# Layer 1 of a two-layer backbone block: the low parts of the way-out weights on one engine, and the first FFN way-out weights loaded into another tile

## The chip, the cores and the metric

The kernel runs on one core of a Trainium2 chip. The metric is the device time of one execution in microseconds (us). Below, TensorE is PE in the profile, with its weight loads as PEld; VectorE is DVE, ScalarE is ACT, GpSimd is POOL, and SyncE, whose queue issues nearly all the transfers, is SP.

## The reference

The block has two layers. Each is a mixer followed by a SwiGLU feed-forward net (FFN), and each of the two starts with an RMS norm whose scale and shift, like the gate on its output, come from a conditioning vector. 512 latent tokens and 256 context tokens pass through layer 0; layer 1 returns the latent tokens only. The model width is 1024, the FFN's hidden width 2816. The change lies in layer 1, from the mixer's output projection (the way out) to the beginning of the FFN:

```python
def finish(o):                                   # o: differential attention, 8 heads of 128
    o = _rms(o, subln_w) * (1.0 - lam_init)
    return o.reshape(o.shape[0], o.shape[1], -1) @ w_out
...
x = x + gx1 * ax                                 # ax = finish(o)
x = x + gx2 * _swiglu(_rms(x, norm_ffn_w[l]) * (1.0 + scx2) + shx2, ffn_w_in[l], ffn_w_out[l])

def _swiglu(h, w_in, w_out):
    gate, up = jnp.split(h @ w_in, 2, axis=-1)
    return (jax.nn.silu(gate) * up) @ w_out
```

## The kernel before

All products are made in three passes of reduced precision. Both operands are split into a high part (a cast) and a low part (the value minus the high part), and TensorE adds high by high, high by low and low by high. So each weight tile of 128x1024 takes three steps, all in `unit` (lines 302 to 311): SyncE loads it into a raw tile (line 305), ScalarE casts it to the high part (line 309), and another engine subtracts to get the low part (line 310). The raw tiles come from a ring of two (`raw_tile`, tag `raw`), so each load waits until the raw tile two loads earlier has been subtracted. High and low parts go into rings of eight (`whi`, `wlo`).

The code is not executed in its written order. A scheduler sets the order of the instructions on each engine and of the loads on SyncE's queue, when the program is built. Within an engine the order is then fixed: an instruction that waits holds up all behind it.

**End of layer 1's mixer.** The last head (h == 7) runs over four tiles of 128 tokens. `attend1` makes the scores `sc`, their maximum (line 643, DVE), the exponentials `e` (line 645, ACT), mixes two of them (lines 651 and 652, DVE), transposes the result (`ppt`, PE), and multiplies by the values (`av`). The head's output `o` is normed: sum of squares (line 672, ACT), a factor `rs_o` in two GpSimd steps (lines 148 and 149, in `rsqrt`), and the multiplication (line 674, DVE). While this head runs, the eight way-out weight tiles are made by `out_units`: raw tiles `wor`, parts `woh` and `wol`. Before the change their subtractions go to GpSimd and VectorE in turn, and every third raw tile has a room of its own (`opa`). `OutProj.operand` transposes `o` (`opt`, line 707), casts it into `hT` (line 708) and subtracts (line 709). `OutProj.sums` runs 24 matmuls for each half of a token tile (`ops`, lines 717 to 719). The four tiles' sums, the gated residual (lines 412 and 413) and the norms of the FFN (`norm_steps`) follow.

**The norms.** For each tile, `norm_steps` writes x times its norm factor into `nroom0` (line 278), transposes it on TensorE (`npt`, line 283, eight 128x128 blocks), applies scale and shift into `nroom1` (line 291 on DVE for the first four blocks, line 289 on ACT for the other four), and splits that into `hT` (cast at line 293; subtraction at line 294, on DVE and on GpSimd). `nroom0` and `nroom1` hold two token tiles each; they are tiles with the tags `hTc0` and `hTc1`, the place of the context's operand, which layer 1's FFN does not need.

**Start of layer 1's FFN.** The hidden columns go in 11 pairs of 128 columns. A pair p loads six weight tiles in this order: two of the gate (`wgr`), two of the up part (`wur`), two of the way out (`wdr`), all through the ring of two raw tiles before the change. For p == 0 the matmuls into `pg` and `pu` (line 750) go in two halves of 256 tokens, so that the first half can start before the norms of the last two tiles are done. Then ScalarE makes `sg` (silu, line 775), DVE multiplies (`pu`, line 777), and the product is split into `hdh` (ACT, line 418) and `hdl` (DVE, line 419) for the way-out matmuls `dps` (lines 799 to 801). Beside that, the gate row of the FFN is made once: a transpose on TensorE (`gps`, line 237), a copy on DVE (`grow`, line 239), a store to DRAM (`gmem`, line 242) and a load back as a 128x1024 tile (`g0`, line 244).

Of the kernel before, what the change touches and what calls it, by code (L numbers as in the profile page):

```python
# [10 lines left out]
F32 = mybir.dt.float32  # L11
# [7 lines left out]
P = 128  # L19
D = 1024  # L20
# [44 lines left out]
def backbone(es: ExitStack, tc: tile.TileContext, x, c, ctx, c_ctx, mod_w, mod_b, norm_mix_w, norm_ffn_w,  # L65
# [3 lines left out]
    nc = tc.nc  # L69
# [3 lines left out]
    keep = es.enter_context(tc.tile_pool(name="keep", bufs=1))  # L73
# [20 lines left out]
    def acc_tile(name, n=512, one=None):  # L94

        if one is None:
            one = turn["acc"] = 1 - turn["acc"]
        return p_1.tile([P, 512], F32, name=name, tag=f"acc{one}")[:, :n]
# [6 lines left out]
    def f32(ap):  # L105
        return ap.bitcast(F32)
# [143 lines left out]
    def ctx_room(shape, dtype, name):  # L250

        return [keep.tile(shape, dtype, name=f"{name}{j}", tag=f"hTc{j}") for j in range(2)]
# [7 lines left out]
    def cols_T(j, s0, s1):  # L260

        return hT[j][0][:, :, s0:s1] if s1 <= SEQ else hT[j][1][:, :, s0 - SEQ:s1 - SEQ]
# [38 lines left out]
    def unit(pool, views, shape, bufs, name, sub=None, new_tile=raw_tile):  # L301

        raw = new_tile(shape, name + "r")
        for dst, src in views(raw):
            nc.sync.dma_start(dst, src)
        p_hi, p_lo = pool if isinstance(pool, tuple) else (pool, pool)
        hi = p_hi.tile(shape, F32R, name=name + "h", tag="whi", bufs=bufs)
        lo = p_lo.tile(shape, F32R, name=name + "l", tag="wlo", bufs=bufs)
        nc.scalar.copy(hi, raw)  # L309
        (sub or nc.vector).tensor_sub(lo, raw, f32(hi))  # L310
        return hi, lo
# [103 lines left out]
    def split(pool, src, shape, tag, bufs):  # L415
        hi = pool.tile(shape, F32R, name=tag + "h", tag=tag + "h", bufs=bufs)
        lo = pool.tile(shape, F32R, name=tag + "l", tag=tag + "l", bufs=bufs)
        nc.scalar.copy(hi, src)
        nc.vector.tensor_sub(lo, src, f32(hi))
        return hi, lo  # L420
# [256 lines left out]
    def out_units(wp, w_out, subs=(nc.gpsimd,), rooms=(raw_tile,)):  # L677
        ws = []
        for k in range(KT):
            def views(raw, k=k):  # L680
                yield raw, w_out[0, k * P:(k + 1) * P, :]
            ws.append(unit(wp, views, [P, D], 8, "wo", subs[k % len(subs)], rooms[k % len(rooms)]))
        return ws
# [38 lines left out]
    def ffn(l, xs, ntok, wp, fp, done, mods=()):  # L722
# [5 lines left out]
        wo, hid = [], []  # L728
        for p in range(NF // 2):
            def w_in(c0, name):  # L730
                res = []
                for u in range(2):
                    def views(raw, u=u):
                        yield raw, ffn_w_in[l, u * 512:(u + 1) * 512, c0:c0 + 256].rearrange(
                            "(j p) n -> p j n", p=P)
                    res.append(unit(wp, views, [P, 4, 256], 8, name))
                return res
            wg, wu = w_in(p * 256, "wg"), w_in(FFN + p * 256, "wu")
            for j in range(2):
                def views(raw, j=j):  # L740
                    yield raw, ffn_w_out[l, (2 * p + j) * P:(2 * p + j + 1) * P, :]
                wo.append(unit(wp, views, [P, D], 8, "wd"))
            for j in range(2):
                def half(w, ps, sgs):
                    for sg in sgs:
                        for k in range(KT):
                            whi, wlo = (z[:, k % 4, j * P:(j + 1) * P] for z in w[k // 4])
                            for a, b, q in ((whi, 0, 0), (whi, 1, 1), (wlo, 0, 2)):
                                for s0, s1 in sg:
                                    nc.tensor.matmul(ps[:, s0:s1], a, cols_T(b, s0, s1)[:, k, :],  # L750
                                                     start=k == 0 and q == 0, stop=k == KT - 1 and q == 2)

                if p == 0 and ntok == NTX:

                    if j == 0:
                        both = [p_sc.tile([P, 2, 512], F32, name=name, tag="sc") for name in ("pg", "pu")]
                        for s in first_segs:
                            for j in range(2):
                                for w, ps in zip((wg, wu), both):
                                    half(w, ps[:, j], [[s]])  # L760
                        j = 0
                    pg, pu = (z[:, j] for z in both)
                elif p == 0 and j == 0:
                    pg, pu = (p_sc.tile([P, 1024], F32, name=name, tag="sc") for name in ("pg", "pu"))

                    for s in first_segs:
                        half(wg, pg, [[s]])
                        half(wu, pu, [[s]])
                else:
                    pg, pu = (p_sc.tile([P, 1024], F32, name=name, tag="sc") for name in ("pg", "pu"))  # L770
                    half(wg, pg, [segs])
                    half(wu, pu, [segs])
                pg, pu = pg[:, :n_tok], pu[:, :n_tok]
                sg = fp.tile([P, n_tok], F32, name="sg", tag="sg", bufs=1)
                nc.scalar.activation(sg, pg, AF.Silu)

                nc.vector.tensor_mul(pu, sg, pu)  # L777
                hid.append(split(fp, pu, [P, n_tok], "hd", 4))
            for i, mod in enumerate(mods[0] if p == 0 and mods else ()):
                mod_chunk(*mod, lambda shape, name: fp.tile(shape, F32, name=name, tag="mw", bufs=2), fp, f"tr{i % 2}", room=("ma", 4))  # L780
            if p and mods and mods[p]:
                mod_chunks_by_pool(mods[p], fp)
            if g is None:
                g = [gate_row(l, 5, i, fp) for i in range(2 if ntok > NTX else 1)]
            if p == NF // 2 - 2:

                continue
            nj = len(hid)
            for t in CTX_FIRST[:ntok] if ntok > NTX else range(ntok):
                for n in range(2):  # L790
                    if nj > 2:
                        ps = acc_tile("dps")
                    else:
                        turn["sum"] = (turn["sum"] + 1) % 4
                        ps = p_1.tile([P, 512], F32, name="dps", tag=("acc0", "tr0", "acc1", "tr1")[turn["sum"]])
                    for j in range(nj):
                        hh, hl = (z[:, t * P:(t + 1) * P] for z in hid[j])
                        a, b = (z[:, n * 512:(n + 1) * 512] for z in wo[j])
                        nc.tensor.matmul(ps, hh, a, start=j == 0, stop=False)  # L799
                        nc.tensor.matmul(ps, hh, b, start=False, stop=False)  # L800
                        nc.tensor.matmul(ps, hl, a, start=False, stop=j == nj - 1)  # L801
                    residual(xs[t], ps, g[0 if t < NTX else 1], n)
                    if p == NF // 2 - 1:
                        done(t, n)
            wo, hid = [], []
# [28 lines left out]
    wp = Pool("mw0", "right")  # L834
# [29 lines left out]
    ws = weights0(0, wp.pool, nc.vector, start_tile)  # L864
# [17 lines left out]
    for b in range(4):  # L882
# [3 lines left out]
        if b < 3:  # L886
            if b == 1:
                tables0(1, tabs, wp.pool)
            ws = weights0(b + 1, wp.pool, nc.gpsimd)
            proj = in_proj0(b + 1, ws, tabs, wp.pool, (even if b % 2 else odd).pool, (wp if b % 2 else odd).pool)  # L890
            nxt = next(proj)
        if b == 3:
            wp.close()
            even.close()
            wp = Pool("w0", "right")
# [3 lines left out]
        for t in order:  # L899
            for hp in range(2):  # L900
# [4 lines left out]
                if b == 3 and hp == 0 and t == 2:  # L905
                    room = [z[:, 0] for z in ctx_room([P, 1, KT, P], F32, "nroom")]
# [53 lines left out]
    wp = Pool("mw1", "right")  # L960
# [32 lines left out]
    for h in range(8):  # L993
        for t in range(NTX):
            att.push(attend1(h, t, state[h], o_t, nlam, subln, at.pool))
            if h == 7 and t == 0:
                whi.close()
                wp.close()
                wlo.close()
                states[2].close()  # L1000
                states[1].close()
                wp = Pool("w1", "right")
                opa = Pool("opa")
                ws = out_units(wp.pool, od_w_out, (nc.gpsimd, nc.vector), (raw_tile, raw_tile, lambda shape, name:
                               opa.pool.tile(shape, F32, name=name, tag="wor", bufs=1)))
                oproj = OutProj(1, ws, o_t, xs, opa.pool)
            if h == 7 and 0 < t <= 3:
                oproj.operand(t - 1)

                with tc.high_priority(-1000):  # L1010
                    oproj.sums(t - 1, 0, opa.pool, nc.gpsimd)
            emit((h + 1) * NT + 2 + (2, 3, 5, 6)[t])
# [4 lines left out]
    room = ctx_room([P, 2, KT, P], F32, "nroom")  # L1017
# [67 lines left out]
```

## Time and profile before

| | |
|---|---|
| time of the runs | 1824.57 us (median of 3; 1823.11 to 1825.61) |
| profiled execution: time | 1825.45 us |
| profiled execution: span, first to last instruction | 1823.7 us |
| granted TensorE clock, mean | 0.985 |
| busy share: PE, PEld, DVE, ACT, POOL | 96%, 80%, 55%, 45%, 35% |
| first way-out sums (`ops`) of layer 1 | 1369.6 us |
| first FFN matmul of layer 1 (`pg`) | 1437.0 us |
| first `dps` of layer 1 | 1469.1 us |

TensorE is busy for 96% of the span, so a time is won or lost where TensorE waits, or where its granted clock is below 1. The rows that matter are therefore those with an idle time in brackets: it is the time for which the engine stood still ahead of the instruction, and the name behind the arrow is what it waited for. All times in rows are microseconds from the start of the span.

### The profile page before, as it was taken

To read this page: it belongs to the slowest core of one execution; us is meant where nothing else is said; L and a number is where in the kernel's file an instruction comes from. 1 tells how busy PE (TensorE), PEld (TensorE's weight loads), DVE (VectorE), ACT (ScalarE), POOL (GpSimd) and SP (SyncE) were. 2 spreads that over 40 slices of the span, in tenths; PEclk is the share of its full clock that TensorE was granted. 3 is DMA by queue.
4 is the path that set the end of the run, shared out by engine and by line. 5 is a ranking of instruction groups with operands and counts; after the bars stand their busy time and mean duration, and the time that the engine had idled before them with its cause. 6 is when DMAs were issued, how large, how long until landed. Compare 5 with 4: busy or idle time off the path is not lost. (4 is left out here: it accounts for less than half of the span.)

```text
span 1823.7 us, 26198 instructions
## 1 busy us (share of the span) xinstructions
PE 1752.0 (96%) x9958; PEld 1458.2 (80%) x9958; DVE 1002.0 (55%) x1703; ACT 825.5 (45%) x1726; POOL 641.8 (35%) x840
## 2 busy tenths in 40 slices
PE   6999999999999999999999899999998999999998
PEld 4877676667888888888888789999986888888886
DVE  4664545443355555545552657777675455655652
ACT  6555555544354444333331656666664532222220
POOL 2764554632053443222220466666643200000000
PEclk8999999999999999999999899999999999999999
DMA  9111322302543334334330311111103233232221
GB/s 314 46 44 55 96 73 99 131 13 76 180 149 117 103 104 140 115 127 126 117 105 3 102 35 59 44 45 44 42 25 104 90 97 102 82 104 93 93 93 47
DMA packets 152478, 165.65 MB, mean 91 GB/s; under 512 B 16480, under 2 KB 139936, under 8 KB 152352
## 3 DMA queue, kind: packets, MB, share of 16 engines
q1 hardware_dynamic: 152000, 163.77, 28.1%
q8 instruction: 78, 1.28, 0.3%
q14 instruction: 48, 0.39, 0.1%
q10 hardware_dynamic: 352, 0.21, 0.0%
HBM read 159.73 MB, written 4.22 MB: 90 GB/s over the span
## 5 line engine op out<-in xcount | busy, mean ns | idle before, releaser
L750 PE MATMUL pg<-hT,wgh 128*128 128x512 f32 (+1 forms) x736 | 244.8, 386 | 2.2 <-ACT hT L293 2.2
L750 PE MATMUL pu<-hT,wuh 128*128 128x512 f32 (+1 forms) x736 | 244.1, 385 | 0.0
L412 DVE TENSOR_TENSOR dps<-dps,g 128x512 f32<-128x512 f32 x200 | 135.7, 697 | 131.3 <-PE dps L801 126.7
L799 PE MATMUL dps<-wdh,hdh 128*128 128x512 f32 x440 | 176.2, 401 | 5.3 <-DVE x L413 3.5
L800 PE MATMUL dps<-wdl,hdh 128*128 128x512 f32 x440 | 174.0, 396 | 0.0
L801 PE MATMUL dps<-wdh,hdl 128*128 128x512 f32 x440 | 166.4, 396 | 0.0
L750 PEld LDWEIGHTS pg<-hT,wgh 128*128 128x128 f32 x736 | 137.2, 189 | 32.7 <-ACT hT L293 2.4
L750 PEld LDWEIGHTS pu<-hT,wuh 128*128 128x128 f32 x736 | 137.1, 189 | 28.5
L750 PE MATMUL pg<-hT,wgl 128*128 128x512 f32 (+1 forms) x368 | 141.9, 386 | 0.0
L750 PE MATMUL pu<-hT,wul 128*128 128x512 f32 (+1 forms) x368 | 141.5, 384 | 0.0
L413 DVE TENSOR_TENSOR x<-x,dps 128x512 f32<-128x512 f32 x200 | 133.3, 683 | 3.3
L405 PE MATMUL inps<-wih,hT 128*128 128x384 f32 x384 | 133.1, 347 | 0.4 <-ACT qkv L451 0.2
L406 PE MATMUL inps<-wil,hT 128*128 128x384 f32 x384 | 130.6, 340 | 0.0
L407 PE MATMUL inps<-wih,hT 128*128 128x384 f32 x384 | 130.6, 340 | 0.0
L198 ACT ACTIVATE modw<-modw,cols 128x256 f32<-128x256 f32 x192 | 81.9, 498 | 69.4 <-DMA modw<-in_mod_w_dram 66.4
L799 PEld LDWEIGHTS dps<-wdh,hdh 128*128 128x128 f32 x440 | 82.7, 188 | 27.6 <-DVE x L413 4.4
L310 DVE TENSOR_TENSOR wul<-wur,wuh 128x1024 fp32r<-128x1024 f32 x44 | 54.6, 1241 | 89.3 <-ACT wuh L309 89.3
L801 PEld LDWEIGHTS dps<-wdh,hdl 128*128 128x128 f32 x440 | 82.6, 188 | 20.2 <-issue 0.4
L750 PE MATMUL pg<-hTc,wgh 128*128 128x256 f32 x352 | 98.3, 283 | 0.5 <-ACT hTc L293 0.2
L750 PE MATMUL pu<-hTc,wuh 128*128 128x256 f32 x352 | 98.2, 282 | 0.0
L800 PEld LDWEIGHTS dps<-wdl,hdh 128*128 128x128 f32 x440 | 82.8, 188 | 17.6
L777 DVE TENSOR_TENSOR pu<-sg,pu 128x768 f32<-128x768 f32 (+1 forms) x44 | 36.5, 829 | 108.3 <-PE pu L750 94.4
(235 smaller groups left out, 4306.3 us busy)
## 6 DMA issues: line engine op xcount, KB each, us to landing
modw<-in_mod_w_dram SPq DMA_DIRECT2D x96, 512.0 KB, 4.0
wgr<-in_ffn_w_in_dram SPq DMA_DIRECT2D x44, 512.0 KB, 3.4
wur<-in_ffn_w_in_dram SPq DMA_DIRECT2D x44, 512.0 KB, 3.4
wdr<-in_ffn_w_out_dram SPq DMA_DIRECT2D x44, 512.0 KB, 3.5
wir<-in_od_w_in_dram SPq DMA_DIRECT2D x96, 128.0 KB, 2.3
x<-in_x_dram SPq DMA_DIRECT2D x8, 512.0 KB, 3.9
wir<-in_ev_w_in_dram SPq DMA_DIRECT2D x16, 256.0 KB, 2.7
wor<-in_ev_w_out_dram SPq DMA_DIRECT2D x8, 512.0 KB, 4.4
```

Source lines behind the costliest of these rows:

```text
L198: nc.scalar.activation(pr[:, k], w[:, k], AF.Copy, scale=cols[:, kk:kk + 1])
L310: (sub or nc.vector).tensor_sub(lo, raw, f32(hi))
L405: nc.tensor.matmul(ps, hs[0][:, k, :], a, start=k == 0, stop=False)
L406: nc.tensor.matmul(ps, hs[0][:, k, :], b, start=False, stop=False)
L407: nc.tensor.matmul(ps, hs[1][:, k, :], a, start=False, stop=k == KT - 1)
L412: nc.vector.tensor_mul(tmp, ps, g[:, n * 512:(n + 1) * 512])
L413: eng.tensor_add(xt[:, n * 512:(n + 1) * 512], xt[:, n * 512:(n + 1) * 512], tmp)
L750: nc.tensor.matmul(ps[:, s0:s1], a, cols_T(b, s0, s1)[:, k, :], start=k == 0 and q == 0, stop=k == KT - 1 and q == 2)
L777: nc.vector.tensor_mul(pu, sg, pu)
L799: nc.tensor.matmul(ps, hh, a, start=j == 0, stop=False)
L800: nc.tensor.matmul(ps, hh, b, start=False, stop=False)
L801: nc.tensor.matmul(ps, hl, a, start=False, stop=j == nj - 1)
```

## The change

Two edits. In `out_units` for layer 1, all eight subtractions that give `wol` go to GpSimd. In `ffn`, the two `wdr` tiles of pair p == 0 of layer 1 are loaded into tiles with the tags `hTc0` and `hTc1`, the place of `nroom0` and `nroom1`, and not into the ring of raw tiles. Three lines are added, so line numbers above 742 are higher by 3 in the changed kernel.

```diff
@@ ffn @@
             for j in range(2):
                 def views(raw, j=j):
                     yield raw, ffn_w_out[l, (2 * p + j) * P:(2 * p + j + 1) * P, :]
-                wo.append(unit(wp, views, [P, D], 8, "wd"))
+
+                room = (lambda shape, name, j=j: keep.tile(shape, F32, name=name, tag=f"hTc{j}")) if l and p == 0 \
+                    else raw_tile
+                wo.append(unit(wp, views, [P, D], 8, "wd", None, room))
@@ backbone, layer 1, h == 7 and t == 0 @@
                 opa = Pool("opa")
-                ws = out_units(wp.pool, od_w_out, (nc.gpsimd, nc.vector), (raw_tile, raw_tile, lambda shape, name:
+                ws = out_units(wp.pool, od_w_out, (nc.gpsimd,), (raw_tile, raw_tile, lambda shape, name:
                                opa.pool.tile(shape, F32, name=name, tag="wor", bufs=1)))
```

The scheduler makes a new order out of this, in two places.

**GpSimd, during the last head.** Before, between the weights' subtractions of the third and the later tiles, the two steps of the first token tile's norm factor (`rs_o_14293`, for head 7) stand together behind two subtractions:

```order
L310 TENSOR_TENSOR wol_14206<-wor_14203,woh_14205 128x1024
L310 TENSOR_TENSOR wol_14218<-wor_14215,woh_14217 128x1024
L148 TENSOR_SCALAR rs_o_14293<-oss_14290 128x1
L149 TENSOR_TENSOR rs_o_14293<-rs_o_14293,neghalf_92 128x1
L310 TENSOR_TENSOR wol_14230<-wor_14227,woh_14229 128x1024
```

In the changed kernel the same stretch of GpSimd reads:

```order
L310 TENSOR_TENSOR wol_14206<-wor_14203,woh_14205 128x1024
L310 TENSOR_TENSOR wol_14212<-wor_14209,woh_14211 128x1024
L310 TENSOR_TENSOR wol_14218<-wor_14215,woh_14217 128x1024
L148 TENSOR_SCALAR rs_o_14293<-oss_14290 128x1
L310 TENSOR_TENSOR wol_14224<-wor_14221,woh_14223 128x1024
L149 TENSOR_TENSOR rs_o_14293<-rs_o_14293,neghalf_92 128x1
L310 TENSOR_TENSOR wol_14230<-wor_14227,woh_14229 128x1024
L310 TENSOR_TENSOR wol_14236<-wor_14233,woh_14235 128x1024
```

The factor's second step now has four subtractions ahead of it, one of them between its two steps. Another subtraction (`wol_14200`, the second tile) stands earlier, right behind the first.

**SyncE and ScalarE, at the start of the FFN.** Before, SyncE's queue has the loads of pair 0's way out (`wdr_14854`, `wdr_14860`) ahead of pair 1's gate (`wgr_15154`, `wgr_15160`) and up part (`wur_15166`, `wur_15172`):

```order
L305 DMA wdr_14854<-in_ffn_w_out_dram 128x1024
L305 DMA wdr_14860<-in_ffn_w_out_dram 128x1024
L305 DMA wgr_15154<-in_ffn_w_in_dram 128x4x256
L305 DMA wgr_15160<-in_ffn_w_in_dram 128x4x256
L305 DMA wur_15166<-in_ffn_w_in_dram 128x4x256
L242 DMA gmem_15078<-grow_15076 8x128
L244 DMA g0_15080<-gmem_15078 128x1024
L305 DMA wur_15172<-in_ffn_w_in_dram 128x4x256
```

and in the changed kernel:

```order
L305 DMA wgr_15154<-in_ffn_w_in_dram 128x4x256
L305 DMA wgr_15160<-in_ffn_w_in_dram 128x4x256
L305 DMA wdr_14854<-in_ffn_w_out_dram 128x1024
L242 DMA gmem_15078<-grow_15076 8x128
L244 DMA g0_15080<-gmem_15078 128x1024
L305 DMA wdr_14860<-in_ffn_w_out_dram 128x1024
L305 DMA wur_15166<-in_ffn_w_in_dram 128x4x256
L305 DMA wur_15172<-in_ffn_w_in_dram 128x4x256
```

Pair 0's way out has moved behind pair 1's gate, and its second tile behind the gate row's store and load. On ScalarE, from the norm of the last tile (`nroom0`) to the first `hdh`, the order before is:

```order
L278 ACTIVATE nroom0_14710<-x3_14640,rs_n_14798 128x1024
L309 CAST wdh_14862<-wdr_14860 128x1024
L309 CAST wgh_15156<-wgr_15154 128x1024
L289 ACTIVATE nroom1_14711<-npt_14813,modc1_107,aff1_109 128x128 x4
L293 CAST hT0_110<-nroom1_14711 128x4x128
L309 CAST wgh_15162<-wgr_15160 128x1024
L293 CAST hT0_110<-nroom1_14711 128x4x128
L309 CAST wuh_15168<-wur_15166 128x1024
L309 CAST wuh_15174<-wur_15172 128x1024
L775 ACT_TABLE_LOAD
L775 ACTIVATE sg_15060<-pg_14866 128x512
L418 CAST hdh_15063<-pu_14867 128x512
```

and in the changed kernel:

```order
L278 ACTIVATE nroom0_14710<-x3_14640,rs_n_14798 128x1024
L289 ACTIVATE nroom1_14711<-npt_14813,modc1_107,aff1_109 128x128 x4
L293 CAST hT0_110<-nroom1_14711 128x4x128 x2
L309 CAST wdh_14856<-wdr_14854 128x1024
L309 CAST wdh_14862<-wdr_14860 128x1024
L309 CAST wgh_15156<-wgr_15154 128x1024
L309 CAST wgh_15162<-wgr_15160 128x1024
L778 ACT_TABLE_LOAD
L778 ACTIVATE sg_15060<-pg_14866 128x512
L309 CAST wuh_15168<-wur_15166 128x1024
L418 CAST hdh_15063<-pu_14867 128x512
```

The last tile's norm now stands ahead of the four weight casts, and the first `hdh` behind one cast of pair 1's up part instead of two. DVE's subtractions of the same tiles follow in the same order (`wdl`, `wdl`, `wgl`, `wgl`), and on TensorE five `pu` matmuls of pair 0 moved from ahead of the last two `npt` groups to behind them.

## The prediction

> **What bounds the kernel now.** I read the table of stretches first, then TensorE's timeline for its idle times, then the timelines of the engines that it waited for. The stretches (length; busy time of PE, PEld, DVE, ACT and POOL; granted clock; DMA):
>
> ```profile
> span 1823.7 us, 26198 instructions
> ...
> 1381.50:1387.10 5.60, 5.60 (x18) 4.63 (x19) 2.39 (x3) 1.92 (x4) 2.17 (x1) 0.50 0.63 204
> ...
> 1453.50:1459.00 5.50, 5.48 (x24) 5.25 (x25) 1.92 (x2) 1.43 (x2) 1.80 (x1) 0.50 0.61 174
> 1459.00:1467.50 8.50, 8.50 (x74) 8.45 (x73) 2.45 (x2) 3.74 (x4) 0.00 (x0) 1.00 0.29 94
> 1467.50:1471.00 3.50, 2.01 (x10) 1.54 (x9) 2.47 (x4) 2.26 (x4) 0.00 (x0) 1.00 0.76 254
> 1471.00:1790.00 319.00, 319.00 (x1369) 256.66 (x1368) 182.65 (x239) 78.07 (x94) 0.00 (x0) 1.00 0.28 89
> ```
>
> From 1471 to 1790 us TensorE works 319.00 of 319 us at clock 1.00: there nothing but TensorE's own work counts. Ahead of it, two stretches ran at half clock. The 74 matmuls in the 8.50 us of full clock give 0.115 us for one of 256 tokens. TensorE's timeline (start, duration, and in brackets the idle time before and its releaser):
>
> ```profile
> 1379.77 0.33 PE L707 MATMUL opt<-cst,o 128*128 128x128 f32 x1 [2.16 <-DVE o L674]
> 1381.50 1.11 PE L659 MATMUL ppt<-cst,e 128*128 128x128 f32 x4 [1.41 <-DVE hT L709]
> 1382.27 0.78 PE L717 MATMUL ops<-woh,hT 128*128 128x512 f32 x1
> ...
> 1388.94 0.60 PE L659 MATMUL ppt<-cst,e 128*128 128x128 f32 x4
> ...
> 1448.47 1.04 PE L283 MATMUL npt<-cst,nroom 128*128 128x128 f32 x8
> ...
> 1451.05 0.28 PE L237 MATMUL gps<-cst,modc 128*8 128x128 f32 x1 [0.95 <-DVE nroom L291]
> 1453.52 0.58 PE L750 MATMUL pg<-hT,wgh 128*128 128x256 f32 x1 [2.20 <-ACT hT L293]
> ...
> 1469.14 0.50 PE L799 MATMUL dps<-wdh,hdh 128*128 128x512 f32 x1 [1.49 <-ACT hdh L418]
> ```
>
> Two places matter. At the way out, TensorE waits 2.16 and 1.41 us, then runs 5.60 us at half clock, a loss of 2.8. At the FFN's start it waits 0.95 and 2.20 us and then loses 2.75 of 5.50 us. A third wait, 1.49 us ahead of the first `dps` at 1469.14, leaves the clock at 1.00 in the stretch around it (1467.5 to 1471).
>
> **The change, part one: `wol` on GpSimd.** The first wait ends with `o` of token tile 0 (L674), which needs the norm factor that GpSimd makes. GpSimd's timeline there:
>
> ```profile
> 1358.23 2.36 POOL L310 TENSOR_TENSOR wol<-wor,woh 128x1024 fp32r<-128x1024 f32 x1 [2.35 <-ACT woh L309]
> ...
> 1365.50 0.56 POOL L149 TENSOR_TENSOR rs_o<-rs_o,neghalf 128x1 f32<-128x1 f32 x1
> ...
> 1372.06 5.78 POOL L310 TENSOR_TENSOR wol<-wor,woh 128x1024 fp32r<-128x1024 f32 x2 [2.75 <-ACT woh L309]
> 1377.92 0.19 POOL L148 TENSOR_SCALAR rs_o<-oss 128x1 f32<-128x1 f32 x1
> 1378.20 1.13 POOL L149 TENSOR_TENSOR rs_o<-rs_o,neghalf 128x1 f32<-128x1 f32 x1
> ```
>
> and VectorE's:
>
> ```profile
> 1371.04 0.22 DVE L651 SCALAR_TENSOR_TENSOR rt<-sm,nlam,rc 128x1 f32<-128x1 f32 x1
> 1371.29 1.02 DVE L652 SCALAR_TENSOR_TENSOR e<-e,rt 128x768 f32<-128x768 f32 x1
> ...
> 1373.09 2.52 DVE L310 TENSOR_TENSOR wol<-wor,woh 128x1024 fp32r<-128x1024 f32 x1
> ...
> 1376.63 1.22 DVE L651 SCALAR_TENSOR_TENSOR rt<-sm,nlam,rc 128x1 f32<-128x1 f32 x1
> ...
> 1379.36 0.35 DVE L674 SCALAR_TENSOR_TENSOR o<-o,rs_o,subln 128x128 f32<-128x128 f32 x1 [0.44 <-POOL rs_o L149]
> ```
>
> A subtraction takes 2.36 us on GpSimd undisturbed. Two together took 5.78 us, while VectorE's own took 2.52; and L651, 0.22 us elsewhere, took 1.22 and ended at 1377.85, when GpSimd's pair ended (1372.06 + 5.78). The two engines took turns, one whole instruction at a time. The Trainium skill has this rule ("SBUF — State Buffer", section "Who interferes with whom"): a VectorE instruction with two SBUF inputs and a GpSimd instruction that reads SBUF exclude each other for their full length. By that rule alone, four such instructions fewer on VectorE are a gain; the sum with it would be the second rival's. The order decides otherwise.
>
> GpSimd now has three subtractions ahead of the factor's first step, a fourth ahead of its second. The first starts at 1372.06 as before, since its raw tile and its cast come as before. Three end at 1372.06 + 3 x 2.36 = 1379.14. VectorE's L651 and L652, held until then, take 0.22 + 1.02: 1380.38. The fourth then ends at 1382.74 and the second step (0.56 when alone) at 1383.30. L674 follows, and the last `opt` 0.41 us behind its start, as now (1379.36 to 1379.77): 1383.71, where before it came at 1379.77. Ahead of the next sums stand that transpose (0.33) and ScalarE's cast of it:
>
> ```profile
> 1381.12 0.58 ACT L708 CAST hT<-opt 128x512 fp32r<-128x512 f32 x1
> ...
> 1450.51 1.04 ACT L309 CAST wgh<-wgr 128x1024 fp32r<-128x1024 f32 x1 [2.06 <-DMA wgr<-in_ffn_w_in_dram]
> 1451.46 1.50 ACT L289 ACTIVATE nroom<-npt,modc,aff 128x128 f32<-128x128 f32 x4
> 1452.84 0.62 ACT L293 CAST hT<-nroom 128x512 fp32r<-128x512 f32 x1
> ...
> 1463.38 1.05 ACT L309 CAST wuh<-wur 128x1024 fp32r<-128x1024 f32 x1 [8.45 <-PE pg L750]
> ...
> 1465.85 1.28 ACT L775 ACT_TABLE_LOAD   x1
> ...
> 1468.51 0.58 ACT L418 CAST hdh<-pu 128x512 fp32r<-128x512 f32 x1 [0.76 <-DVE pu L777]
> ```
>
> 0.58 us, with some 0.1 for the hand-overs: 1384.7, where before they began at 1382.27: +2.4 us. One group of transposes (1388.94, about 0.4 us to the next matmul) that was due soon after now stands behind the next sums: -0.4. I take **+2.0 us** for part one. If VectorE's pair doesn't hold the fourth subtraction, it is 1.2 less; and the half clock behind the wait can end a good microsecond earlier or later in TensorE's work than now. Hence 0 to +3. GpSimd's last two subtractions end at about 1388; the sums that need them come later, so they cost nothing, and neither do the FFN's first raw tiles behind them, which `pg` needs at 1437.0 (the small table).
>
> **Part two: the norm of the last token tile.** In ScalarE's rows, the cast of `wgr` waited 2.06 us for its load, and the norm's scale and shift (L289, 1451.46) stood behind it. This cover for the norm is gone: the order has no weight cast ahead of it, and on VectorE no `wdl`:
>
> ```profile
> 1448.49 1.23 DVE L310 TENSOR_TENSOR wdl<-wdr,wdh 128x1024 fp32r<-128x1024 f32 x1 [1.44 <-ACT wdh L309]
> ...
> 1452.73 0.27 DVE L239 COPY grow<-gps 8x128 f32<-8x128 f32 x1
> 1453.50 0.69 DVE L294 TENSOR_TENSOR hT<-nroom,hT 128x512 fp32r<-128x512 f32 x1 [0.50 <-ACT hT L293]
> ```
>
> Five `pu` matmuls (0.6 us) move behind the transposes, which start at 1447.9 and end after 1.04 us at 1448.95. L289 takes 1.50 us, the first cast (L293) 0.62: `pg` can start at about 1451.1. Until then TensorE has ten `pu` matmuls, to 1450.1, and the short `gps`. The wait is 1.0 us, then 0.4 more for VectorE's L294 (0.69, two matmuls beside it), in place of 0.95 + 2.20. Waits of 1.49 and less have not lowered the clock, so the 2.75 us go too. The remaining 94 of this half's 96 matmuls end at 1451.75 + 94 x 0.115 = 1462.55, where before they ended 1.49 us ahead of 1469.14: 1467.65.
>
> **Part three: what is late next.** `hdh` of the first 128 columns stands on ScalarE behind the cast of `wuh_15168`. Before, that cast waited for TensorE (8.45 us, at 1463.38); now it waits for a load that has a long chain ahead of it, through SyncE's queue:
>
> ```profile
> 1453.30 0.35 SPq L242 DMA_DIRECT2D gmem<-grow  x1
> 1456.35 0.34 SPq L244 DMA_DIRECT2D g<-gmem  x1
> 1456.78 0.39 SPq L305 DMA_DIRECT2D wur<-in_ffn_w_in_dram  x1
> ```
>
> and the loads' median time from issue to landing, the last column of the DMA table:
>
> ```profile
> wur<-in_ffn_w_in_dram SPq DMA_DIRECT2D x44, 512.0 KB, 3.4
> wdr<-in_ffn_w_out_dram SPq DMA_DIRECT2D x44, 512.0 KB, 3.5
> ...
> g<-gmem SPq DMA_DIRECT2D x6, 512.0 KB, 4.9
> ```
>
> `gps` ends at 1450.35 and `grow` (0.27) follows at once; the store `gmem` was issued 0.57 us after the start of `grow`: 1450.9. The load `g` comes 3.05 us after the store (1453.30 to 1456.35), the next issue 0.43 later: the second `wdr` at 1454.4. It lands 3.5 us later: 1457.9. Then `wdh` (1.05), `wdl` and `wgl` on VectorE (1.23 each) free the raw tile at 1461.4; ScalarE's two `wgh` casts (1.04 each), the table load (1.28) and `sg` fit in beside that. The load of `wur_15166` lands 3.4 us later: 1464.8. Its cast (1.05) and `hdh` (0.58) end at 1466.45; **`dps` starts at 1466.5, 2.6 us earlier than now**. But TensorE has then waited from 1462.55, 4.0 us, longer than the waits that lowered the clock twice above. I charge the same half clock behind it, 2.75 us: net **+0.1 us** for parts two and three. Its bounds: loads at 4.9 us (the gate row's median, for it moves as many bytes right ahead) would put `dps` 2.9 us later, and no half clock would take 2.75 off.
>
> Behind that, nothing is short: the six loads of a pair stay in the same ring, and 319 us without a gap stand over them.
>
> **The sum** is 2.0 + 0.1 = +2.1 us. It is made in an execution of 1825.45 us, 0.88 above the runs' median; put on the median of 1824.57 it gives 1826.7 us. About 0.2% (3.65 us) is what a measurement of this kernel can tell from no change.
>
> **The rivals.**
>
> *The load chain is later than reckoned (slower).* The second `wdr` runs beside the gate row's load, and its delay passes through four engines to `hdh`. With 4.9 us for `wdr` and for `wur`, `dps` starts at 1469.4, as late as now, with the half clock on top: 0.3 + 2.75 + 2.0 = +5.0 us, 1829.6 us. It decides from 1.55 us on, that is from a `dps` later than 1468.05 (2.1 + 1.55 = 3.65). For it: the two transfers are 1 MB together. Against it: the medians of 3.5 and 3.4, over 44 loads each.
>
> *GpSimd's chain costs nothing and VectorE's relief counts (faster).* If the factor came no later than now, the 2.16 + 1.41 us and the 2.8 us behind them would go: -6.4 + 0.1 = -6.3 us, 1818.3 us. For it: VectorE's 2.52 us and 1.22 us. Against it: four subtractions stand ahead of the factor's second step, and 4 x 2.36 us behind 1372.06 is past 1381.5 already.
>
> *The clock stays up at 1462 us.* Then the 2.75 us are not lost: -2.6 + 2.0 = -0.6 us, 1824.0 us. For it: the wait of 1.49 us lowered nothing. Against it: 0.95 + 2.20 us, with a transpose between, did. A rule of the Trainium skill speaks for this rival ("TensorE: Matmul & The Clock Gate", section "What's actually happening"): the clock is halved after an idle window of about 3.4 us, and the windows run freely. By it, a wait of 4.0 us would seldom hold a whole window; the trace shows the drop after less.
>
> **How the numbers follow.** The forecast case has 0.47, the late chain 0.28, the clock that stays up 0.15, the relief 0.10. Faster by over 0.2% is the relief alone: 0.10. Slower is the late chain and a little of the forecast's upper end: 0.30. The rest, 0.60, is within 0.2%. The range goes from 1821 us (part one at 0 and no half clock, -2.6, and a microsecond for what the sum leaves out) to 1831 us (the late chain with part one at +3, 1830.6); it leaves out the relief and what lies past the late chain.
>
> **What would show it.** Right: GpSimd's `rs_o` for tile 0 ends after 1382.5 us and `opt` follows; the wait ahead of `pg` at about 1451 us shrinks under 1.5 us with no half clock behind; `dps` starts after a wait of 3 to 5 us for ScalarE's `hdh`, with the clock at 0.50 behind. Wrong: a wait at the way out no longer than now, or a `dps` that starts right behind the last `pu`; then the kernel is faster.

## The result, and the profile after

The changed kernel takes 1830.66 us (median of 5 runs, 1827.80 to 1835.14) against 1823.11 us for the kernel before (median of 5): a ratio of 1.0041, with a 95% interval of 1.0029 to 1.0053, so +7.5 us (5.3 to 9.7). A second measurement (experiment 5) gives +6.4 us. It is slower by 0.4%. My number was 1826.7 us, +2.1.

The profiled execution of the changed kernel took 1835.14 us, 9.7 more than that of before. Not all of this is the change. The first row below is TensorE's last long wait ahead of the stretch that the change reorders, at `qpt` of the last head, in the kernel before; behind it come TensorE's rows of the changed kernel. The timeline of the kernel before:

```profile
1355.15 0.37 PE L619 MATMUL qpt<-identr,qd 128*128 128x128 f32 x2 [2.38 <-ACT qd L606]
```

TensorE's timeline of the changed kernel (start, duration, idle time before and its releaser):

```profile
1358.36 0.50 PE L619 MATMUL qpt<-identr,qd 128*128 128x128 f32 x2 [2.38 <-ACT qd L606]
...
1385.97 1.11 PE L659 MATMUL ppt<-cst,e 128*128 128x128 f32 x4 [4.09 <-DVE hT L709]
1390.52 0.48 PE L707 MATMUL opt<-cst,o 128*128 128x128 f32 x1 [3.43 <-DVE o L674]
1391.67 0.79 PE L717 MATMUL ops<-woh,hT 128*128 128x512 f32 x1 [0.68 <-ACT hT L708]
...
1459.70 0.38 PE L753 MATMUL pg<-hT,wgh 128*128 128x256 f32 x1 [0.81 <-ACT hT L293]
...
1475.39 0.80 PE L802 MATMUL dps<-wdh,hdh 128*128 128x512 f32 x1 [3.63 <-ACT hdh L418]
```

The changed kernel is 3.21 us late at `qpt` already, where both kernels still do the same: that is the spread of executions. So I count from `qpt`. The last `opt` of token tile 0 comes 32.16 us behind it, where before it came 24.62 us behind (1379.77 - 1355.15): +7.5. The first `ops` row behind that `opt`, "the sums" from here on, comes at 33.31 against 27.12: **+6.2**. (The `ops` rows ahead of it, from 1369.6 us on before, don't need the last head.) `pg` comes at 101.34 against 98.37: only +3.0 is left. `dps` comes at 117.03 against 113.99: +3.0. At the kernel's last wait of TensorE, at 1811.30 us, it is +6.0, because a half clock lies behind the first `dps`, as the table of stretches shows (length; busy time of PE, PEld, DVE, ACT and POOL; granted clock; DMA):

```profile
1391.67:1395.64 3.97, 3.97 (x10) 3.08 (x11) 1.10 (x2) 0.44 (x1) 1.01 (x1) 0.51 0.79 280
1459.70:1471.70 12.00, 11.78 (x96) 11.43 (x96) 5.39 (x5) 6.35 (x7) 1.28 (x1) 1.00 0.38 117
1475.39:1481.40 6.01, 6.01 (x15) 4.76 (x16) 4.55 (x6) 3.13 (x4) 0.00 (x0) 0.54 0.56 164
```

The 4.09 us ahead of `ppt` are no loss of their own here: `opt`, which stands behind it, had to wait until 1390.52 anyway. The FFN did about what was forecast: the half clock behind `pg` is gone (1.00 over 96 matmuls), a wait of 3.63 us ahead of `dps` and a half clock behind it have come. The loss came at the way out. GpSimd's timeline of the changed kernel there:

```profile
1376.32 7.76 POOL L310 TENSOR_TENSOR wol<-wor,woh 128x1024 fp32r<-128x1024 f32 x3 [1.18 <-ACT woh L309]
1384.17 0.19 POOL L148 TENSOR_SCALAR rs_o<-oss 128x1 f32<-128x1 f32 x1
1384.79 2.71 POOL L310 TENSOR_TENSOR wol<-wor,woh 128x1024 fp32r<-128x1024 f32 x1 [0.43 <-ACT woh L309]
1387.46 0.55 POOL L149 TENSOR_TENSOR rs_o<-rs_o,neghalf 128x1 f32<-128x1 f32 x1
1387.97 4.70 POOL L310 TENSOR_TENSOR wol<-wor,woh 128x1024 fp32r<-128x1024 f32 x2
```

and VectorE's:

```profile
1376.45 2.30 DVE L651 SCALAR_TENSOR_TENSOR rt<-sm,nlam,rc 128x1 f32<-128x1 f32 x1
1378.79 3.09 DVE L652 SCALAR_TENSOR_TENSOR e<-e,rt 128x768 f32<-128x768 f32 x1
...
1384.01 0.22 DVE L651 SCALAR_TENSOR_TENSOR rt<-sm,nlam,rc 128x1 f32<-128x1 f32 x1
1384.26 1.02 DVE L652 SCALAR_TENSOR_TENSOR e<-e,rt 128x768 f32<-128x768 f32 x1
...
1388.04 2.42 DVE L674 SCALAR_TENSOR_TENSOR o<-o,rs_o,subln 128x128 f32<-128x128 f32 x1 [2.12 <-POOL rs_o L149]
```

The factor (`rs_o`, L149) is ready at 1388.01, 29.65 us behind `qpt`, where before it was ready 24.18 us behind: +5.5. And then L674, the step that uses it, takes 2.42 us in place of 0.35: GpSimd had started the next subtraction at 1387.97, 0.07 us ahead of L674, and held VectorE for the whole of it. 5.5 + 2.1 is the +7.5 of `opt`. The first pair of rows (L651 and L652 of the token tile ahead of the last) is held too, for 4.15 us together; free, they take 0.22 and 1.02, as the second pair does.

A part of the 5.5 is chance, not the change. TensorE's granted clock in the 12 us behind `qpt` was 0.86 before and 0.59 in the changed kernel. Experiment 5 is the changed kernel again, in an execution with 0.86 there: its factor is ready 27.50 us behind `qpt` (+3.3), its L674 takes 2.43 us, its `opt` comes at 30.02 (+5.4) and its sums at 31.17 (**+4.05**). Before, in the table of stretches (the third number from the end is the clock):

```profile
1355.15:1367.15 12.00, 11.03 (x66) 9.12 (x67) 9.65 (x18) 9.21 (x20) 3.59 (x5) 0.86 0.26 87
```

Before, GpSimd's pair of subtractions began when L652 of that tile was already running (1372.06, in a row from 1371.29 on), and not ahead of L651. It follows ScalarE's casts, and these follow the loads, whose order on SyncE's queue is another one. The queue's timeline before:

```profile
1366.39 0.29 SPq L242 DMA_DIRECT2D gmem<-grow  x1
1366.73 0.34 SPq L305 DMA_DIRECT2D wor<-in_od_w_out_dram  x1
```

and in the changed kernel:

```profile
1363.96 3.13 SPq L305 DMA_DIRECT2D wor<-in_od_w_out_dram  x3
1372.52 0.29 SPq L242 DMA_DIRECT2D gmem<-grow  x1
```

Before, the third of these `wor` loads stood behind the store of the mixer's gate row. Now the store stands behind it. ScalarE's timeline, before:

```profile
1370.94 2.94 ACT L309 CAST woh<-wor 128x1024 fp32r<-128x1024 f32 x3 [1.04 <-DMA wor<-in_od_w_out_dram]
```

and in the changed kernel:

```profile
1375.21 2.94 ACT L309 CAST woh<-wor 128x1024 fp32r<-128x1024 f32 x3
```

The casts waited 1.04 us for the load before, and wait for nothing now; that wait had let L651 and L652 pass first. The other executions bear this out: where the casts wait for that load (experiments 2, 7, 10 and 12, by 0.76 to 1.17 us), L652 of this tile takes 1.02 us; where they don't (1, 4, 5, 9 and 11), it takes 3.08 to 3.10.

### The profile page after: what moved, and what is told of

Same layout as the page of the kernel before. It is cut to its first block, busy times and chain, and to the rows that moved or that the text cites. A ratio compares the mean times of both kernels' runs of the same rounds, so it can differ in the third digit from the quotient of the medians.

```text
span 1833.4 us, 26196 instructions
## 1 busy us (share of the span) xinstructions
PE 1755.9 (96%) x9958; PEld 1463.0 (80%) x9958; DVE 999.9 (55%) x1699; ACT 826.2 (45%) x1726; POOL 651.4 (36%) x844
```

## The experiments

Three theories. **A**: the loss lies at the way out, by GpSimd's subtractions. It has two branches: **A1**, VectorE's two-input steps are held while they run; **A2**, the norm factor stands behind them in GpSimd's row. **B**: it lies in the load chain at the FFN's start. **C**: it is where the clock's half-speed stretches fell in these executions. (**D** and **E** come with experiment 7.) Each difference below is the ratio of five rounds to the runs of the kernel before on the same chip, with its 95% interval, times that kernel's median (1824 to 1825 us).

**1. Part one alone.** Edit: `out_units(..., (nc.gpsimd,), ...)`, the FFN as before.

> Part one alone: all eight low parts of layer 1's way-out weights on GpSimd, the FFN's loads as before. Theory A (the loss lies at the way out: GpSimd's subtractions hold VectorE's two-input steps L651, L652, L674 and stand ahead of the norm factor): +5 to +7 us against the kernel before, with the way out's first sums 5 us or more later. Theory B (my prediction's sizes; the loss lies at the FFN's load chain): +2 us, at most +3. Theory C (neither part; the clock's windows fall differently from run to run): within +-2 us and rounds that differ by more than that.

Measured: 1.0027 (1.0015 to 1.0040), **+4.9 us** (2.7 to 7.3). TensorE's timeline:

```profile
1355.63 0.50 PE L619 MATMUL qpt<-identr,qd 128*128 128x128 f32 x2 [2.39 <-ACT qd L606]
...
1387.86 0.48 PE L707 MATMUL opt<-cst,o 128*128 128x128 f32 x1 [3.43 <-DVE o L674]
1389.01 0.79 PE L717 MATMUL ops<-woh,hT 128*128 128x512 f32 x1 [0.68 <-ACT hT L708]
```

The sums come 33.38 us behind `qpt`, as in the changed kernel. The total lies just under theory A's 5 to 7 us, and its interval reaches down into theory B's 2 to 3. The sums decide for A: by B they would come some 2 us later than before, and they come 6.3 us later (4.05 with equal clocks, above).

**2. Part two alone.** Edit: the `room` for the `wdr` tiles of pair 0; subtractions of the way out in turn, as before.

> Part two alone: the first raw way-out tiles of the FFN in the norms' room, the subtractions alternating as before. Theory A: -1 to +1.5 us, the wait ahead of pg shrinks from 0.95 + 2.20 us to under 1.5 us and a wait of 3 to 4 us ahead of the first dps takes its place. Theory B: +5 us or more, with the wait ahead of dps as the loss. Theory C: as theory A, but no sum of the two parts gives the +7.5 us of both.

Measured: 1.0007 (0.9994 to 1.0019), **+1.3 us** (-1.1 to 3.5). Theory B, which expected 5 us or more of this part, falls. The wait has moved to `dps`, with half clock behind it (0.80 us for a matmul that takes 0.50), in TensorE's timeline:

```profile
1467.82 0.80 PE L802 MATMUL dps<-wdh,hdh 128*128 128x512 f32 x1 [3.75 <-ACT hdh L418]
```

The two parts add up to +6.2 us, against +7.5 and +6.4 for both: the totals don't need C.

**3. The opposite of part one.** Edit: `out_units(..., (nc.vector,), ...)`.

> The opposite of part one: all eight low parts on VectorE (the rest as before). If GpSimd's subtractions cost by standing ahead of the factor and by holding VectorE (theory A), GpSimd now makes its factor at once and nothing holds L651 and L652, but four more subtractions of about 1.2 us stand in VectorE's own row: between -4 and +2 us. Theory B and C, for which who subtracts matters little: -2 to +2 us.

Measured: 0.9995 (0.9986 to 1.0003), **-0.9 us** (-2.6 to 0.5), no difference that the runs can tell. Four subtractions more on VectorE cost nothing that shows; four more on GpSimd cost 4.9 us.

**4. VectorE's relief alone.** Edit: VectorE's four of the eight subtractions left out (these units take the low part of the unit ahead); GpSimd keeps its four. The call, without the few lines in `unit` that go with it:

```diff
-ws.append(unit(wp, views, [P, D], 8, "wo", subs[k % len(subs)], rooms[k % len(rooms)]))
+ws.append(unit(wp, views, [P, D], 8, "wo", subs[k % len(subs)], rooms[k % len(rooms)],
+               ws[-1][1] if len(subs) == 2 and k % 2 else None))
```

> VectorE's relief without GpSimd's load: the four low parts that VectorE computed are left out (those four units use the low part of the unit ahead), GpSimd keeps its four as before. Theory A: -1 to -5 us, since VectorE has four instructions less and GpSimd none more; what e1 loses against this kernel is then GpSimd's alone. Theories B and C: 0 +-2 us.

Measured: 1.0003 (0.9993 to 1.0013), **+0.5 us** (-1.3 to 2.4). The relief is worth nothing that shows, though theory A expected 1 to 5 us of it. VectorE's timeline says where it went (the line numbers are higher by 3: L654 and L655 are L651 and L652):

```profile
1372.52 2.30 DVE L654 SCALAR_TENSOR_TENSOR rt<-sm,nlam,rc 128x1 f32<-128x1 f32 x1
1374.86 3.10 DVE L655 SCALAR_TENSOR_TENSOR e<-e,rt 128x768 f32<-128x768 f32 x1
```

With only two subtractions in that place on GpSimd, the pair is held as long as in the changed kernel.

That makes this kernel the counterpart of experiment 1. In both, VectorE makes no low part of the way-out weights and the pair is held for the same time, and the clock in the 12 us behind `qpt` was the same (0.57 here, 0.58 there). They differ in the four subtractions that experiment 1 gives to GpSimd. TensorE's timeline of this execution, whose `qpt` starts at 1354.29:

```profile
1382.83 0.79 PE L721 MATMUL ops<-woh,hT 128*128 128x512 f32 x1 [0.68 <-ACT hT L712]
```

The sums come 28.54 us behind `qpt` here and 33.38 there: 4.8 us, and 4.4 us in the totals (4.9 - 0.5). So the held pair, which both have, is not what makes the 4.4 us. That is GpSimd's longer row, with the late factor and the held L674 behind it.

**5. The changed kernel again.**

> The changed kernel once more, beside the runs below. Part one alone measured +4.9 us (2.7 to 7.3), part two alone +1.2 us (-1.1 to +3.5). Theory A (the parts add): +6 us, from +4 to +8. Theory C (a part of the +7.5 us was where the clock's windows fell in those runs): below +4 us.

Measured: 1.0035 (1.0024 to 1.0045), **+6.4 us** (4.4 to 8.2), as theory A expected. This execution's sums come 31.17 us behind `qpt` (1383.24 - 1352.07). With 33.31 and 33.38 above the mean is 32.6. The executions with the old order of the way out have 27.12 (before) and 28.62 (experiment 2). The clock behind `qpt` was not the same in all: 0.59, 0.58 and 0.86 in the new order, 0.86 and 0.72 in the old one. At 0.86 part one puts the sums 4.05 us later (31.17 against 27.12).

**6. Smaller pieces.** Edit: each subtraction of part one in four pieces of 256 columns.

```diff
-(sub or nc.vector).tensor_sub(lo, raw, f32(hi))
+for c in range(cut):
+    w = ...                                    # a quarter of the columns
+    (sub or nc.vector).tensor_sub(lo[w], raw[w], f32(hi)[w])
```

> Part one alone with each of GpSimd's eight subtractions cut into four pieces of 256 columns (the row order of GpSimd is the same, with four pieces where one stood). Theory A1 (the loss is VectorE held for whole GpSimd instructions: L651 and L652 took 2.30 and 3.10 us in place of 0.22 and 1.02, L674 2.42 in place of 0.34): VectorE gets in between pieces, L651 + L652 under 2.6 us and L674 under 1.0 us; +1 to +3 us against the kernel before in place of +4.9. Theory A2 (the loss is the factor's place behind the subtractions in GpSimd's row): the pieces change nothing, +4 to +7 us.

Measured: 1.0038 (1.0025 to 1.0050), **+6.9 us** (4.6 to 9.1). GpSimd's timeline:

```profile
1373.73 9.73 POOL L313 TENSOR_TENSOR wol<-wor,woh 128x256 fp32r<-128x256 f32 x12 [1.18 <-ACT woh L309]
...
1386.54 0.55 POOL L149 TENSOR_TENSOR rs_o<-rs_o,neghalf 128x1 f32<-128x1 f32 x1
```

and VectorE's (L655 is L652, L677 is L674):

```profile
1374.52 1.46 DVE L655 SCALAR_TENSOR_TENSOR e<-e,rt 128x768 f32<-128x768 f32 x1
...
1387.12 0.81 DVE L677 SCALAR_TENSOR_TENSOR o<-o,rs_o,subln 128x128 f32<-128x128 f32 x1 [5.70 <-POOL rs_o L149]
```

The holds shrink as A1 expected, and nothing is gained: L674 loses 1.6 us less, but twelve pieces take 9.73 us where three whole subtractions took 7.75 (VectorE gets in between them more often), and the factor comes 1.85 us later behind `qpt` than in experiment 1 (31.56 against 29.71). A1 alone falls; the factor's place counts.

**7. Part two, with the gate row out of SyncE's queue.** Edit on experiment 2: the FFN's `gmem` and `g0` go through `nc.gpsimd.dma_start`.

> Part two alone, with the FFN's gate row stored and loaded by GpSimd's DMA queue, so that the second raw way-out tile doesn't stand behind the row's store and load in SyncE's queue. In part two alone that load was issued 4.2 us after the first, and the first dps waited 3.75 us and then ran at half clock (some 2.7 us more). Theory D (the prediction's chain: store, load, second wdr, its casts, the next wur, hdh): the wait falls under 1 us, the half clock goes, and the kernel takes 4 to 6 us less than part two alone: -5 to -2 us against the kernel before. Theory E (the wait is for the transfers' own time): dps waits 3 us or more as before, +1 us.

Measured: 0.9994 (0.9982 to 1.0005), **-1.1 us** (-3.3 to 0.9). Theory D (the chain through the gate row's store and load) expected a wait under 1 us, no half clock and 2 to 5 us gained; theory E (the transfers' own time) a wait of 3 us or more. Neither came. TensorE's timeline:

```profile
1465.34 0.80 PE L803 MATMUL dps<-wdh,hdh 128*128 128x512 f32 x1 [2.16 <-ACT hdh L419]
```

The wait is 2.16 us in place of 3.75, so the gate row was a part of it, and the half clock stays. GpSimd's and SyncE's timelines show what I had missed, the room itself:

```profile
1451.81 1.30 POOL L295 TENSOR_TENSOR hT<-nroom,hT 128x512 fp32r<-128x512 f32 x1
```

```profile
1453.14 0.34 SPq L306 DMA_DIRECT2D wdr<-in_ffn_w_out_dram  x1
```

The second raw tile lies where `nroom1` lay, and its load can't start until GpSimd's last subtraction of the norm has read that (1451.81 + 1.30 = 1453.11). What the gate row had cost was mostly in the transfer: from issue to cast the second `wdr` takes 4.92 us behind the gate row's load (experiment 2, 1454.16 to 1459.08) and 3.52 where that load isn't ahead of it in the queue (1453.14 to 1456.66).

**8. Experiments 3 and 7 together.**

> The same with all eight subtractions of the way out on VectorE. Theories A and D: what e3 (-0.9 us) and the run above give together, -6 to -3 us. Theory E: within 1.5 us of the kernel before.

Measured: 0.9991 (0.9979 to 1.0004), **-1.6 us** (-3.8 to 0.7). The 3 to 6 us that theories A and D expected did not come. It isn't shown to be faster than the kernel before; it is faster than the changed kernel (+6.4 us on the same chip).

**9 and 10. The two halves of part one.** Edits: engines of `out_units` listed by unit, with units 1 and 7, or 3 and 5, moved to GpSimd.

> Half of part one: only units 1 and 7 go over to GpSimd, 3 and 5 stay on VectorE. GpSimd's row then has two subtractions ahead of token tile 0's factor, as before, and two instead of one behind it. Theory A2 (the loss is the factor's place behind the subtractions): -1 to +1.5 us. Theory A1 (VectorE held by GpSimd's instructions, wherever they stand): half of part one, +2 to +3 us.

> The other half: only units 3 and 5 go over; three subtractions then stand ahead of the factor's first step and a fourth ahead of its second, as in the changed kernel, and one behind it. Theory A2: all or nearly all of part one's loss, +3 to +6 us. Theory A1: half of it, +2 to +3 us.

Measured: 1.0016 (1.0004 to 1.0027), **+2.9 us** (0.7 to 4.9), and 1.0016 (1.0007 to 1.0025), **+2.9 us** (1.3 to 4.6). The totals fit A1's half and half, and both together (+5.8) agree with the whole (+4.9); but the interval of the first overlaps A2's -1 to +1.5 us, and that of the second A2's 3 to 6. The executions show that the halves lose in two ways. With units 1 and 7, GpSimd's and VectorE's timelines:

```profile
1372.73 4.73 POOL L310 TENSOR_TENSOR wol<-wor,woh 128x1024 fp32r<-128x1024 f32 x2 [1.17 <-ACT woh L309]
```

```profile
1375.19 3.08 DVE L652 SCALAR_TENSOR_TENSOR e<-e,rt 128x768 f32<-128x768 f32 x1
```

In this kernel the loads have changed places, and so L652 is held. The factor isn't what is late; VectorE makes its next low part behind L652, and TensorE's timeline shows the wait for it:

```profile
1379.46 0.80 PE L718 MATMUL ops<-wol,hT 128*128 128x512 f32 x1 [3.31 <-DVE wol L310]
```

The whole of part one has no such wait, since there VectorE makes no low part. With units 3 and 5, VectorE's timeline:

```profile
1372.38 1.02 DVE L652 SCALAR_TENSOR_TENSOR e<-e,rt 128x768 f32<-128x768 f32 x1
...
1384.14 2.42 DVE L674 SCALAR_TENSOR_TENSOR o<-o,rs_o,subln 128x128 f32<-128x128 f32 x1 [2.43 <-POOL rs_o L149]
```

Here that L652 is free, but the factor is late and L674 is held. The sums come 28.44 us behind `qpt` with units 1 and 7 (clock 0.86; 27.12 before, with the same clock) and 32.92 with units 3 and 5 (clock 0.72; 28.62 in experiment 2, with the same clock): +1.3 and +4.3. At the sums, then, it is A2's half that loses most. Where the rest of the +2.9 us of units 1 and 7 arises, this execution doesn't show.

**11 and 12. No factor.** Edit on part one, and on the kernel before: `r = rsqrt(...) if h < 7 else ss`, which leaves out the last head's norm factor; L674 multiplies by the sum of squares itself.

> Part one alone, with the norm factor of the last head left out (VectorE's L674 multiplies by the sum of squares itself), so that nothing of the way out waits for GpSimd's row but the last low parts. Theory A2: no later than the next kernel, the same without part one, -1 to +1.5 us between the two. Theory A1: +3 to +5 us between the two, since L651, L652 and L674 are held as before.

> The kernel before, with the last head's norm factor left out in the same way: what the one above is compared with. By the profile of before, the wait of 2.16 us ahead of opt was for that factor: -1 to -4 us against the kernel before by both theories.

Measured: 0.9986 (0.9975 to 0.9997), -2.6 us, and 0.9964 (0.9949 to 0.9979), **-6.6 us** (-9.3 to -3.8), more than the 1 to 4 us expected: 4.0 us between the two, where A2 allowed 1.5 and A1 expected 3 to 5. But at the sums only 1.4 us of it stands (26.67 us behind `qpt` against 25.24, with clocks of 0.72 and 0.74); with the factor it was 4.05. The rest comes at the FFN's start, where experiment 11 waits 1.91 us ahead of `pg` and experiment 12 doesn't wait. Leaving the factor out changes the program's order there too (in experiment 12, SyncE loads a `wur` tile ahead of the gate row), so the totals don't settle A1 against A2. At the way out the pair says what experiments 1 and 4 say: the factor's way, L674's hold included, carries most of it (2.6 of 4.05 us).

## Why the prediction was wrong in size, step by step

The direction was right; slower by more than 0.2%, to which I gave 0.30, is what happened, and my likeliest case, +2.1 us, was too small by 4.3 to 5.4 us. The time lies inside the range, 1821 to 1831 us, by luck: its upper end was made of a late load chain with part one at +3, and that is not what came.

- *Part one, +2.0 us (0 to +3)*: the step that failed, in its size. It measured +4.9 us in time. At the sums, where the prediction had +2.4 (1384.7 against 1382.27), it is +4.05 between the two executions with the same clock behind `qpt` (before, and experiment 5). The mechanism was the one named: three subtractions ahead of the factor's first step, a fourth ahead of the second, and `opt` waiting for it. Three things were wrong in it. (1) "L674 follows, and the last `opt` 0.41 us behind its start": L674 has two inputs in SBUF as L651 has, the subtraction behind the factor in GpSimd's row starts at the same moment, and L674 took 2.42 us. That is 2.1 us, and I had quoted both the rule and the row that say it. The Trainium skill's rule ("SBUF — State Buffer", section "Who interferes with whom") agrees with the held rows shown here. (2) From the start of the first of these subtractions to the factor it takes 11.7 us in the changed kernel and in experiments 1 and 5, where I had 11.24 (1372.06 to 1383.30): 0.4 us. The three subtractions took 7.75 us, not 7.08, since VectorE takes turns between them, and the fourth waited 0.43 us for its cast. (3) "The first starts at 1372.06 as before, since its raw tile and its cast come as before": the load's place in SyncE's queue had changed. With the same clock behind `qpt` the first now starts 1.1 us earlier (15.81 us behind `qpt` in experiment 5, 16.91 before), and so ahead of the pair L651, L652 of the tile ahead, which is held for 4.15 us. I had counted a hold for the last tile alone. 2.4 + 2.1 + 0.4 - 1.1 is 3.8 of the 4.05 us at the sums.
- *Part two, the wait ahead of `pg`*: right. 0.81 and 0.23 us, reckoned 1.0 and 0.4, with the clock at 1.00.
- *Part three, `dps`*: right. A wait of 3.63 us (3.59 and 3.75 in experiments 5 and 2), reckoned 4.0, with a half clock behind. From the gate row's store to `dps` it took 16.15 us, reckoned 15.6 (1450.9 to 1466.5). Inside that, two sizes were off and nearly cancelled, which was luck. SyncE's timeline of the changed kernel:

```profile
1459.24 0.30 SPq L242 DMA_DIRECT2D gmem<-grow  x1
...
1461.77 0.37 SPq L305 DMA_DIRECT2D wdr<-in_ffn_w_out_dram  x1
```

  and ScalarE's:

```profile
1466.80 1.05 ACT L309 CAST wdh<-wdr 128x1024 fp32r<-128x1024 f32 x1 [4.63 <-DMA wdr<-in_ffn_w_out_dram]
...
1473.81 1.04 ACT L309 CAST wuh<-wur 128x1024 fp32r<-128x1024 f32 x1 [2.15 <-DMA wur<-in_ffn_w_in_dram]
```

  The second `wdr` was issued 2.53 us behind the store, where I had 3.5. Its room had come free only 0.24 us before (at 1461.53, behind GpSimd's last subtraction of the norm), and I had left the room out. Its transfer took 5.03 us to the cast, the 4.9 of the slower rival and not 3.5. `wur` took 3.54 us from its issue (1470.27), reckoned 3.4.
- *Net of parts two and three, +0.1 us*: from the sums to the last wait of the kernel it takes 419.80 us before, 419.63 in the changed kernel, 420.32 and 420.03 in experiments 2 and 5: between -0.2 and +0.5.
- *The rivals*: the late chain would have given 1829.6 us, near the time that came, but for a reason that isn't the one that came. The relief of VectorE is worth nothing that shows (experiment 4). The clock did not stay up behind `dps`.

What stays open: whether the change also lowers the clock behind `qpt`. In the four profiled executions with the lowest clock there, 0.57 to 0.59 (the changed kernel, experiments 1, 4 and 6), the loads stand in the new order; the seven with the old order have 0.72 to 1.00. But experiments 5, 9 and 11, in the new order, have 0.72 to 0.86 too, and one execution each is too few to tell. And what the held L651 and L652 cost by themselves is not shown: in the changed kernel their delay is hidden behind the factor's, and in experiment 4 it stands against VectorE's relief.

## What to carry to other kernels

An elementwise step moved from VectorE to GpSimd can cost more than its place in GpSimd's row. In these traces the VectorE steps with two SBUF inputs that started just behind a GpSimd subtraction lasted past its end, and the dearest was the consumer of GpSimd's own result (2.42 us in place of 0.35), because another subtraction stood right behind that result. So look in the new order for what GpSimd starts next when its result is awaited, and for loads that have changed places with something else in their queue. A tile borrowed from an earlier stage brings that stage's last reader with it; in experiment 7 that set the start of the second load, 4.0 us behind the first (1449.17 to 1453.14).

## What the runs showed of the hardware that was not expected

Whether a wait of TensorE is followed by half clock is, in these traces, not a matter of its length alone. In experiment 7 a wait of 2.16 us was followed by half clock (0.80 us a matmul, above); in experiment 12 one of 2.54 us was not, in TensorE's timeline:

```profile
1457.21 0.50 PE L799 MATMUL dps<-wdh,hdh 128*128 128x512 f32 x1 [2.54 <-ACT hdh L418]
```

And the half clock lasts for unequal times: behind the same wait of 2.38 us at `qpt`, two executions of the changed kernel have these 12 us, in the table of stretches; the profiled one first, experiment 5 second:

```profile
1358.36:1370.36 12.00, 10.89 (x49) 9.24 (x50) 6.44 (x11) 7.52 (x16) 5.54 (x6) 0.59 0.38 125
```

```profile
1352.07:1364.07 12.00, 10.77 (x67) 9.20 (x68) 8.32 (x17) 9.17 (x20) 5.92 (x6) 0.86 0.39 131
```

0.27 of 12 us is 3.2 us of TensorE's work. That is of the size of the runs' spread (the kernel before took 1819.0 to 1829.9 us over the 30 runs beside experiments 9 to 12), though no run shows that it is the cause. The rule of the Trainium skill ("TensorE: Matmul & The Clock Gate", section "What's actually happening") that the windows run freely fits this. Its length for an idle window, about 3.4 us, doesn't show here: one wait of 2.16 us was followed by half clock.
